# Second preparation of a chunked RWKV-7 layer with doubled buffers, group norm per tile, and another layout of pools and PSUM banks

## The chip, the cores and the metric

The kernel runs on one core of a Trainium2 chip. The metric is device time in microseconds (us), the median of several executions. Engines: PE multiplies matrices (PEld is its weight load), DVE is the vector engine, ACT the scalar engine, POOL is GpSimd, SP issues nearly all DMA transfers, in one queue.

## The reference, cut to what matters

The whole is one inference step of two layers: an RWKV-7 time mixing, a gated MLP, a windowed attention, a second gated MLP. Only the time mixing is touched, and the projection behind it:

```
r, k, v, decay, a, g = projections of the normed input        # g: gate, low rank, weights g1, g2
y, S_T = wkv7_scan(r, decay, k, v, -kk, kk * a, S0)           # 512 prompt tokens from S0 = 0,
                                                              # and 8 sample sequences of 4 tokens from given states
y = (y - mean) * rsqrt(var + eps)                             # group norm, per token and head of 64
y = y * ln_w + ln_b + sum(r * k * r_k) * v                    # the bonus
out = (y * g) @ w_o                                           # then x = x + out, and a norm
```

## The kernel before, in words

The 544 tokens (32 of the samples, 512 of the prompt) are two groups: group 0 has 288 columns (the first 256 prompt tokens and the samples), group 1 has 256. Function `rwkv` (L788) does the time mixing. Its first part makes r, k, v and the low-rank inputs by large matmuls. Then, per group g:

- `prep(g)` (L806) runs eight units, one for each pair of heads, by `unit_prep` (L397). The first half of a unit loads weights (l_raw) and r, k, v (`in0` to `in2`, from the spill), makes two tanh tiles `th0`, `th1` on ACT (L59 is the line of every operation that goes through the wrapper class `Lane`), a scan `cl` on DVE, its exponentials `dx` and `di`, `kk`, then the products `AR` (DVE), `BK` and `BE` (POOL). The second half makes the bonus from `pb` (a tile that shares the buffers of `cl`; matmul L485), transposes `BE` (L493), multiplies `AR` with `BK` (L498) and masks the result into `G` on DVE. The second half of unit m-1 stands in the program behind the first half of unit m.
- `inverses` (L505) inverts the triangular blocks of `G`: copies, a 32x32 transpose, sixty dependent DVE operations, transposes back, small matmuls.
- `scan(g)` calls `chain` (L561): four chunks of 64 tokens, one after the other through the state S. Per chunk: `own` (L570, matmuls L575, needed for the next chunk), the state's share (L598), `W` (L601, L602), matmuls L606, `UV` (L608, L609), the new state (L617, DVE L622 or L624), and `out` (L579, matmuls L583 and L587, ACT L589 into `yt`).
- `y_norm` (L715) is the group norm of the four `yt` tiles (and, for group 0, of two sample tiles `Ws`): sum and centring on DVE, squares on ACT, sum on DVE; then for all tiles together one scaling and one power -0.5 on POOL (tile `y_var`, 40 or 32 columns), then one POOL multiplication per tile.
- `outputs(g)` calls `y_out` (L740) for four pairs of heads: transposes of `yt` (L746), and for each of eight m the load of the bonus and of a gate weight (`lg_raw`, L759), its split into two parts (`lg_hi` on ACT, `lg_lo` on POOL), three matmuls (L98 to L100), two DVE operations, and a store to a spill in DRAM (`y_spill`, L773).

The order in `rwkv` (from L911 on): scan(0), prep(1) with `samples` (L630, the sample sequences, two halves) put in between, y_norm(0), inverses(1), scan(1), outputs(0), the final states, y_norm(1), outputs(1). Behind it, in `body` (L1527), `y_split` (L776) reads the spill back (`y_in`) and splits it into the operand tiles `y0` and `y1`, and a `Projection` (L945) multiplies by w_o: all eight blocks of group 0, a norm, all eight of group 1. Then the MLP.

The program is written in that order, but a scheduler with a timing model of its own fixes the order on each engine: what is ready may go ahead of earlier code. `Lane` (L51) bounds this: in each of four streams (even units, odd units, samples, y) an operation is placed only when the one 2 or 3 before it on its engine is done. Each engine and the SP queue then run in their fixed order. A tile name has a number of buffers (`bufs`); buffers of one name go round in the program's order, and a new use waits for the last reader of the old. Pools are stacks, from the left or the right end of SBUF: a pool opened after another was closed lies on its memory, and each of its tiles waits for the tiles that lay there.

Before the change `th0`, `th1`, `cl`, `di`, `kk` and `BK` have one buffer in prep(1); pool `us` (operands of the samples) lies on the left, `sp` (samples) and `yo` (y_norm and y_out) on the right, and behind them the next stage's weights `wp2` and `y0`, `y1`, `y_in` (pool `mp`) lie on the right too, from the same end. PSUM (8 banks): sm 1, cw 1, cp 3, pp 3; in the projection and the MLP pp 2, mm 6.

Of the kernel before, what the change touches and what calls it, by code (L numbers as in the profile page):

```python
# [9 lines left out]
F = mybir.dt.float32  # L10
FR = mybir.dt.float32r
AF = mybir.ActivationFunctionType
OP = mybir.AluOpType
# [54 lines left out]
def run(gen):  # L68
    for _ in gen:
        pass  # L70
# [558 lines left out]

def samples(c, hb, b, sp):  # L630

# [9 lines left out]
    for j in range(4):  # L641
        vk = sp.tile([128, 4, 128], F, name="st", bufs=2)
# [16 lines left out]
    nc.scalar.activation(V, rows(ps), AF.Copy)  # L659
    BE = sp.tile([128, 4, 128], F, name="st", bufs=2)  # L660
    for j in range(4):
# [6 lines left out]
    nc.scalar.activation(BT, rows(ps, 128), AF.Copy)  # L668
    W = sp.tile([128, 4, 64], F, name="Ws", bufs=2)
    ps = c.sm()  # L670
# [14 lines left out]
    WU = sp.tile([128, 4, 64], F, name="WUs", bufs=1)  # L685
    nc.vector.tensor_scalar(WU, W, c.parity[:, 2:3], None, op0=OP.mult)
    U = WU
# [27 lines left out]
def y_norm(c, yt, yo):  # L715

    nc = c.slow[3]
    var = c.small.tile([128, 40], F, name="y_var", bufs=1)
    parts = []
    for t in yt:  # L720
        k = t.shape[1] // 64
        at = parts[-1][2] if parts else 0
        parts.append((t.rearrange("p (x v) -> p x v", v=64), at, at + k))
    for t, lo, hi in parts:
        k = hi - lo
        s = c.small.tile([128, 8], F, name="y_sum", bufs=2)
        nc.vector.reduce_sum(s[:, :k], t, axis=AX.X)
        nc.vector.scalar_tensor_tensor(t, s[:, :k].unsqueeze(2).to_broadcast([128, k, 64]), -1.0 / 64, t,
                                       op0=OP.mult, op1=OP.add)
        sq = yo.tile([128, 8, 64], F, name="y_sq", bufs=1)  # L730
        nc.scalar.activation(sq[:, :k], t, AF.Square)
        nc.vector.reduce_sum(var[:, lo:hi], sq[:, :k], axis=AX.X)
    w = parts[-1][2]
    nc.vector.tensor_scalar(var[:, :w], var[:, :w], 1.0 / 64, 64e-5, op0=OP.mult, op1=OP.add)
    nc.gpsimd.tensor_tensor(var[:, :w], var[:, :w], c.mhalf[:, :w], OP.pow)
    for t, lo, hi in parts:
        nc.gpsimd.tensor_tensor(t, t, var[:, lo:hi].unsqueeze(2).to_broadcast([128, hi - lo, 64]), OP.mult)


def y_out(c, g, jj, yt, ys, yo):  # L740
# [13 lines left out]
    for par in range(2):  # L754
        m = 2 * jj + par
        bn = yo.tile([128, NA], F, name="bonus_in", bufs=2)
        nc.sync.dma_start(bn[:, :n], c.bd[:, m, g0:g0 + n])
        lg = yo.tile([128, 128], F, name="lg_raw", bufs=1)
        nc.sync.dma_start(lg, a["rwkv_g2"][0, :, m * 128:(m + 1) * 128])  # L759
        lhi = yo.tile([128, 128], FR, name="lg_hi", bufs=1)  # L760
        llo = yo.tile([128, 128], FR, name="lg_lo", bufs=1)
        split(c, lhi, llo, lg, nc.gpsimd, nc)
# [25 lines left out]
def rwkv(c):  # L788
    nc, tc, a = c.nc, c.tc, c.a
    with ExitStack() as rx:  # L790
# [51 lines left out]

        px, py, rp, rq, ra, rb = (ExitStack() for _ in range(6))
        pm = px.enter_context(c.pool("ps_mm", space=PSUM))
# [41 lines left out]
        px.close()  # L886
        us = rx.enter_context(c.pool("us"))
        u0 = rx.enter_context(c.pool("u0"))
# [30 lines left out]
        up = rx.enter_context(c.pool("up1"))  # L919
# [5 lines left out]
        sp = rx.enter_context(c.pool("sp", side="right"))  # L925
        yo = rx.enter_context(c.pool("yo", side="right"))
        scan(0)
        p1 = prep(1)
        next(p1)
        for hb in range(2):  # L930
            ysm.append(samples(c, hb, smp[hb], sp))
# [595 lines left out]
def body(tc, a, dbg=None, stop=None):  # L1527
# [7 lines left out]
    with ExitStack() as ctx:  # L1535
# [19 lines left out]
        def layers(layer, pr, rest, end, last=None):  # L1555
            with ExitStack() as px:
                psn = px.enter_context(c.pool("ps2", space=PSUM))
                c.pp = lambda: psn.tile([128, 512], F, name="pp", bufs=2)
                psp = px.enter_context(c.pool("ps3", space=PSUM))
                c.mm = lambda: psp.tile([128, 512], F, name="mm", bufs=6)  # L1560
                if last:
                    c.fin = px.enter_context(c.pool("fin"))
                rest()
                x = pr.x
                dump(c, ("x1", "x3")[layer], x)
                mx.close()
                ffn(c, layer, x, end, last)
                dump(c, ("x2", "x4")[layer], x)
# [101 lines left out]
```

## Time and profile before

| | |
|---|---|
| three runs | 2258.44, 2258.45, 2260.52 us (median 2258.45) |
| the profiled execution, own time | 2257.57 us |
| its span, first to last instruction | 2255.5 us |
| granted TensorE clock, mean | 0.942 of full speed |
| busy over the span | PE 91%, PEld 85%, DVE 52%, ACT 40%, POOL 27% |

The span is cut into stretches in the rows below. A busy share over the whole says little here, since PE is full for most of the time and half idle between about 270 and 593 us, where the time mixing's chains run. A wait is read as: which engine stood idle before an instruction, and what released it.

### The profile page before, as it was taken

The numbers are of one execution on the slowest core, as the hardware profiler recorded it, in microseconds if no ns is written. First come the engines' busy times: TensorE is split into PE (matmuls) and PEld (weight loads), VectorE is DVE, ScalarE is ACT, GpSimd is POOL, SyncE is SP. The second block draws the span as 40 slices with busy tenths as digits, with TensorE's granted clock in tenths as the row PEclk, the third lists the DMA queues.
The fourth block names the chain that finished last, engine by engine and source line by source line (L and its number), as shares of the span: only waits on it lengthen the run. The fifth ranks groups of instructions, "written<-read, shape, count | busy, mean of one in ns | idle before, by whom it ended". The sixth has DMA issues, their size and how long they took to land. (4 is left out here: it accounts for less than half of the span.)

```text
span 2255.5 us, 48553 instructions
## 1 busy us (share of the span) xinstructions
PE 2049.3 (91%) x19286; PEld 1926.7 (85%) x19286; DVE 1173.4 (52%) x2402; ACT 895.2 (40%) x1867; POOL 612.4 (27%) x786
## 2 busy tenths in 40 slices
PE   6889848746699999999899999999999999999998
PEld 5888746535699999999889888888888799999998
DVE  6776876665474443325445445454454664344323
ACT  6555523312354444324333333333333354444323
POOL 5874815523132222002111111111111132222101
PEclk9989968658699999999999999999999999999999
DMA  4236511214542332336444444354444443233233
GB/s 155 90 110 202 154 37 44 56 23 118 149 137 82 90 91 83 96 109 179 122 134 129 127 136 130 106 140 124 127 126 124 135 135 90 82 93 88 86 89 108
DMA packets 445053, 250.15 MB, mean 111 GB/s; under 512 B 43578, under 2 KB 436954, under 8 KB 444698
## 3 DMA queue, kind: packets, MB, share of 16 engines
q1 hardware_dynamic: 444826, 247.05, 38.6%
q8 instruction: 151, 2.47, 0.5%
q14 instruction: 76, 0.62, 0.1%
HBM read 202.74 MB, written 30.85 MB: 104 GB/s over the span
## 5 line engine op out<-in xcount | busy, mean ns | idle before, releaser
L99 PE MATMUL mm<-xn,w_hi 128*128 128x256 f32 (+1 forms) x2688 | 788.8, 294 | 2.0 <-DVE xn L1009 0.9
L98 PE MATMUL mm<-xn,w_hi 128*128 128x256 f32 (+1 forms) x2688 | 784.5, 293 | 3.7 <-ACT xn L1008 3.7
L100 PE MATMUL mm<-xn,w_lo 128*128 128x256 f32 (+1 forms) x2688 | 780.5, 291 | 0.0
L75 DVE TENSOR_TENSOR w_lo<-w_raw,w_hi 128x512 fp32r<-128x512 f32 (+1 forms) x575 | 434.7, 758 | 561.9 <-ACT w_hi L74 550.8
L74 ACT ACTIVATE w_hi<-w_raw 128x512 fp32r<-128x512 f32 (+1 forms) x575 | 355.8, 620 | 551.1 <-PE mm L99 488.7
L98 PEld LDWEIGHTS mm<-xn,w_hi 128*128 128x128 f32 x2688 | 509.4, 190 | 9.9 <-ACT xn L1008 4.3
L99 PEld LDWEIGHTS mm<-xn,w_hi 128*128 128x128 f32 x2688 | 510.0, 190 | 6.9 <-issue 2.8
L100 PEld LDWEIGHTS mm<-xn,w_lo 128*128 128x128 f32 x2688 | 509.0, 190 | 3.1 <-issue 3.0
L98 PE MATMUL mm<-act,w_hi 128*128 128x288 f32 (+1 forms) x704 | 200.6, 289 | 1.6 <-ACT y_out L1041 1.6
L1195 POOL TENSOR_TENSOR qk_raw<-qk_raw,rope 128x1088 f32<-128x1088 f32 x24 | 86.2, 3594 | 420.4 <-DMA qk_sw<-qk_raw 384.1
L99 PE MATMUL mm<-act,w_hi 128*128 128x288 f32 (+1 forms) x704 | 200.1, 288 | 0.0
L100 PE MATMUL mm<-act,w_lo 128*128 128x256 f32 (+1 forms) x704 | 198.9, 289 | 0.0
L98 PEld LDWEIGHTS mm<-act,w_hi 128*128 128x128 f32 x704 | 131.9, 189 | 1.7 <-ACT y_out L1041 1.7
L99 PEld LDWEIGHTS mm<-act,w_hi 128*128 128x128 f32 x704 | 131.6, 188 | 0.0
L147 POOL TENSOR_TENSOR acc<-acc,sq_t 128x288 f32<-128x288 f32 (+1 forms) x56 | 46.7, 834 | 310.8 <-ACT sq_t L146 310.7
L100 PEld LDWEIGHTS mm<-act,w_lo 128*128 128x128 f32 x704 | 130.8, 188 | 0.0
L100 PE MATMUL mm<-mx,w_lo 128*128 128x288 f32 (+1 forms) x384 | 114.3, 300 | 3.4 <-DVE w_lo L75 3.3
L98 PE MATMUL mm<-mx,w_hi 128*128 128x288 f32 (+1 forms) x384 | 114.1, 299 | 1.7 <-ACT w_hi L74 1.6
L99 PE MATMUL mm<-mx,w_hi 128*128 128x288 f32 (+1 forms) x384 | 113.5, 297 | 0.0
L100 PEld LDWEIGHTS mm<-mx,w_lo 128*128 128x128 f32 x384 | 74.6, 195 | 6.5 <-DVE w_lo L75 5.8
L1280 ACT ACTIVATE scores<-scores,sm_m 128x512 f32<-128x512 f32 (+3 forms) x80 | 50.4, 631 | 72.0 <-DVE sm_m L1279 69.9
L98 PEld LDWEIGHTS mm<-mx,w_hi 128*128 128x128 f32 x384 | 75.1, 196 | 2.8 <-ACT w_hi L74 2.3
(363 smaller groups left out, 3277.5 us busy)
## 6 DMA issues: line engine op xcount, KB each, us to landing
w_raw<-ffn_w_up SPq DMA_DIRECT2D x176, 256.0 KB
w_raw<-attn_w_in SPq DMA_DIRECT2D x144, 256.0 KB
w_raw<-ffn_w_down SPq DMA_DIRECT2D x90, 256.0 KB
w_raw<-rwkv_w_rkv SPq DMA_DIRECT2D x80, 256.0 KB
qk_sw<-qk_raw SPq DMA_DIRECT2D x96, 136.0 KB
cache_k<-cache_k_w SPq DMA_DIRECT2D x96, 128.0 KB
cache_v<-cache_v_w SPq DMA_DIRECT2D x96, 128.0 KB
w_raw<-rwkv_w_o SPq DMA_DIRECT2D x32, 256.0 KB
```

Source lines behind the costliest of these rows:

```text
L74: (nc or c.nc).scalar.activation(out_hi, src, AF.Copy)
L75: lo_engine.tensor_tensor(out_lo, src, out_hi.bitcast(F), OP.subtract)
L98: nc.tensor.matmul(ps, hi, xhi(i), start=first and i == 0, stop=False)
L99: nc.tensor.matmul(ps, hi, xlo(i), start=False, stop=False)
L100: nc.tensor.matmul(ps, lo, xhi(i), start=False, stop=last and i == len(w) - 1)
L147: nc.gpsimd.tensor_tensor(acc, acc, t[:, :n], OP.add)
L1195: nc.gpsimd.tensor_tensor(raw, raw, c.rope[:, 0:1].to_broadcast([128, 2, NT]), OP.mult)
L1280: nc.scalar.activation(s[:, :w], s[:, :w], AF.Exp, scale=0.125, bias=m[:, 1:2], accum_out=m[:, 2:3])
```

## The change

It does the following:

- prep(1) gets two buffers for `th0`, `th1`, `cl`, `di`, `kk` (c.ub) and for `BK` (c.ubk).
- In `samples`: `um` shares the buffers of `st`, which get three instead of two (before: `um` two of its own); `Ws` moves to the longer-lived pool `sa`; the masking `WUs` goes from DVE to ACT.
- `y_norm` does scaling, power and multiplication tile by tile; `var` is a small tile with two buffers.
- `y_out`: bonus_in 4 buffers instead of 2, lg_raw 3 instead of 1, lg_hi and lg_lo 2 instead of 1.
- PSUM in this part: sm 2, `cw` and `cp` together 3, pp 3. The projection gets its own banks in `layers` (mm 5, pp 3, closed before the MLP opens mm 6, pp 2).
- SBUF: `us` goes to the right end; `us`, `sp` and prep(1)'s pool `up1` are closed before y_norm(0), and `yo` is opened after that on the left, where `up1` was.

```diff
-    W = sp.tile([128, 4, 64], F, name="Ws", bufs=2)
+    W = keep.tile([128, 4, 64], F, name="Ws", bufs=2)
...
-    nc.vector.tensor_scalar(WU, W, c.parity[:, 2:3], None, op0=OP.mult)
+    nc.scalar.activation(WU, W, AF.Copy, scale=c.parity[:, 2:3])
...
-        um = sp.tile([128, 8, 64], F, name="um", bufs=2)
+        um = sp.tile([128, 8, 64], F, name="um", tag="st", bufs=3)
...
-        so = sp.tile([128, 4, 128], F, name="st", bufs=2)
+        so = sp.tile([128, 4, 128], F, name="st", bufs=3)
...
+        t = t.rearrange("p (x v) -> p x v", v=64)
+        var = c.small.tile([128, 8], F, name="y_var", bufs=2)[:, :k]
+        s = c.small.tile([128, 8], F, name="y_sum", bufs=2)[:, :k]
+        nc.vector.reduce_sum(s, t, axis=AX.X)
+        nc.vector.scalar_tensor_tensor(t, s.unsqueeze(2).to_broadcast([128, k, 64]), -1.0 / 64, t, op0=OP.mult, op1=OP.add)
         sq = yo.tile([128, 8, 64], F, name="y_sq", bufs=1)
         nc.scalar.activation(sq[:, :k], t, AF.Square)
...
+        nc.vector.reduce_sum(var, sq[:, :k], axis=AX.X)
+        nc.vector.tensor_scalar(var, var, 1.0 / 64, 64e-5, op0=OP.mult, op1=OP.add)
+        nc.gpsimd.tensor_tensor(var, var, c.mhalf[:, :k], OP.pow)
+        nc.gpsimd.tensor_tensor(t, t, var.unsqueeze(2).to_broadcast([128, k, 64]), OP.mult)
...
-        bn = yo.tile([128, NA], F, name="bonus_in", bufs=2)
+        bn = yo.tile([128, NA], F, name="bonus_in", bufs=4)
...
-        lg = yo.tile([128, 128], F, name="lg_raw", bufs=1)
+        lg = yo.tile([128, 128], F, name="lg_raw", bufs=3)
...
-            so = sp.tile([128, 4, 128], F, name="st", bufs=2)
+            so = yo.tile([128, 4, 128], F, name="p_st", bufs=1)
...
-        us = rx.enter_context(c.pool("us"))
+        us = ru.enter_context(c.pool("us", side="right"))
...
-        c.sm = lambda: pq.tile([128, 512], F, name="sm", bufs=1)
-        c.cw = lambda: pq.tile([128, 512], F, name="cw", bufs=1)
-        c.cp = lambda: pq.tile([128, 512], F, name="cp", bufs=3)
+        c.sm = lambda: pq.tile([128, 512], F, name="sm", bufs=2)
+        c.cw = c.cp = lambda: pq.tile([128, 512], F, name="cp", bufs=3)
...
-        c.ubk = 1
+        c.ub, c.ubk = 2, 2
...
         run(p1)
+        ux.close()
+        rs.close()
+        ru.close()
+        yo = rx.enter_context(c.pool("yo"))
         y_norm(c, st[0]["yt"] + ysm, yo)
...
+                with c.pool("ps2", space=PSUM) as psn:
+                    c.mm = lambda: psn.tile([128, 512], F, name="mm", bufs=5)
+                    c.pp = lambda: psn.tile([128, 512], F, name="pp", bufs=3)
+                    rest()
```

## Rows read from the trace of the kernel before

**Rows 1.** Busy us by stretch: PE, PEld, DVE, ACT, POOL; PEclk, DMA share, GB/s.
```profile
318.00:357.00 39.00, 35.14 (x717) 30.99 (x712) 22.94 (x36) 16.64 (x36) 17.73 (x25) 0.95 0.09 20
357.00:467.00 110.00, 83.69 (x431) 62.78 (x430) 63.59 (x103) 36.65 (x80) 66.36 (x89) 0.67 0.26 58
467.00:506.00 39.00, 12.95 (x281) 11.97 (x281) 31.46 (x76) 4.51 (x7) 1.01 (x3) 0.53 0.08 13
506.00:549.00 43.00, 37.18 (x700) 33.25 (x700) 24.93 (x49) 10.87 (x24) 10.02 (x13) 0.87 0.23 68
549.00:593.00 44.00, 13.76 (x46) 9.72 (x44) 12.40 (x24) 6.76 (x15) 13.51 (x13) 0.52 0.56 162
593.00:622.00 29.00, 28.79 (x195) 28.51 (x196) 20.40 (x38) 17.65 (x39) 5.64 (x6) 0.90 0.66 183
622.00:1005.00 383.00, 381.78 (x3041) 381.09 (x3040) 166.28 (x322) 158.25 (x281) 79.99 (x136) 1.00 0.34 98
```

**Rows 2.** Timeline, 547 to 594 us: start, duration, instruction, idle time before and its releaser.
```profile
547.02 1.41 DVE L624 TENSOR_TENSOR S<-cp,SD 64x512 f32<-64x512 f32 x2 [1.59 <-PE cp L617]
...
549.18 0.60 ACT L838 ACTIVATE st<-sm 128x512 f32<-128x512 f32 x1 [0.80 <-PE sm L836]
...
561.28 0.48 PE L746 MATMUL pp<-ca,yt 128*128 128x128 f32 x1 [0.52 <-POOL yt L59]
...
577.40 0.31 ACT L59 ACTIVATE lg_hi<-lg_raw 128x128 fp32r<-128x128 f32 x1 [2.56 <-DMA lg_raw<-rwkv_g]
...
580.23 0.31 ACT L59 ACTIVATE lg_hi<-lg_raw 128x128 fp32r<-128x128 f32 x1 [2.52 <-DMA lg_raw<-rwkv_g]
...
589.53 0.32 SPq L773 DMA_DIRECT2D y_spill<-bonus_in  x1
589.90 0.43 SPq L783 DMA_DIRECT2D y_in<-y_spill  x1
...
593.16 0.85 PE L98 MATMUL mm<-y,w_hi 128*128 128x288 f32 x2 [4.21 <-ACT y L74]
```

**Rows 3.** Groups by line, 549 to 593 us: busy us, mean ns, idle before, releaser.
```profile
L98 PE MATMUL pp<-hg,lg_hi 128*128 128x256 f32 x8 | 4.6, 579 | 16.2 <-ACT lg_hi L59 16.2
...
L59 ACT ACTIVATE lg_hi<-lg_raw 128x128 fp32r<-128x128 f32 x7 | 2.2, 309 | 22.5 <-DMA lg_raw<-rwkv_g 22.5
...
L59 DVE TENSOR_REDUCE y_var<-y_sq 128x8 f32<-128x512 f32 x1 | 0.7, 685 | 0.8 <-ACT y_sq L59 0.8
```

**Rows 4.** Groups by line on POOL, 357 to 467 us (columns as in rows 3).
```profile
L59 POOL TENSOR_TENSOR y_var<-y_var,mhalf 128x40 f32<-128x40 f32 x1 | 6.8, 6772 | 0.0
...
L59 POOL TENSOR_TENSOR BK<-th,di 128x256 f32<-128x256 f32 x7 | 5.1, 732 | 34.6 <-PE pp L498 21.4 <-PE pp L416 13.2
...
L59 POOL TENSOR_TENSOR yt<-yt,y_var 128x512 f32<-128x512 f32 x4 | 4.0, 1032 | 0.0
```

**Rows 5.** Timeline of single instructions in the second preparation (columns as in rows 2).
```profile
370.30 0.47 ACT L59 ACTIVATE th<-pp,hpar 128x256 f32<-128x256 f32 x1 [5.44 <-PE pp L498]
...
428.46 4.04 POOL L59 TENSOR_TENSOR Ss<-Ss,s_dend 128x512 f32<-128x512 f32 x4
...
429.20 4.81 DVE L59 TENSOR_SCALAR WUs<-Ws,cb 128x256 f32<-128x256 f32 x1
...
430.54 0.47 ACT L59 ACTIVATE th<-pp,hpar 128x256 f32<-128x256 f32 x1 [1.15 <-POOL Ss L59]
```

**Rows 6.** Timeline of the first and second scan (columns as in rows 2).
```profile
329.08 1.14 DVE L59 SCALAR_TENSOR_TENSOR yt<-y_sum,yt 128x512 f32<-128x512 f32 x1
...
333.77 1.15 PE L575 MATMUL cw<-UV,G 128*64 128x64 f32 x32
...
337.07 1.39 DVE L624 TENSOR_TENSOR S<-cp,SD 64x512 f32<-64x512 f32 x2 [2.51 <-PE cp L617]
...
337.73 1.10 PE L587 MATMUL cp<-UV,G 128*64 128x64 f32 x32
...
524.98 1.97 PE L575 MATMUL cw<-UV,G 128*64 128x64 f32 x32
```

More of the change, by code (lines that the diff above doesn't have):

```diff
@@ L627, in chain, with samples @@
         out(ch, S)
-def samples(c, hb, b, sp):
+def samples(c, hb, b, sp, keep):
     nc, a = c.slow[2], c.a
@@ L641, in samples @@
     for j in range(4):
-        vk = sp.tile([128, 4, 128], F, name="st", bufs=2)
+        vk = sp.tile([128, 4, 128], F, name="st", bufs=3)
         for x in range(2):
@@ L659, in samples @@
     nc.scalar.activation(V, rows(ps), AF.Copy)
-    BE = sp.tile([128, 4, 128], F, name="st", bufs=2)
+    BE = sp.tile([128, 4, 128], F, name="st", bufs=3)
     for j in range(4):
@@ L717, in y_norm @@
     nc = c.slow[3]
-    var = c.small.tile([128, 40], F, name="y_var", bufs=1)
-    parts = []
     for t in yt:
         k = t.shape[1] // 64
[L722 to L729, printed above, removed]
+        t = t.rearrange("p (x v) -> p x v", v=64)
[3 more added lines that the diff above has]
+        nc.vector.scalar_tensor_tensor(t, s.unsqueeze(2).to_broadcast([128, k, 64]), -1.0 / 64, t, op0=OP.mult, op1=OP.add)
         sq = yo.tile([128, 8, 64], F, name="y_sq", bufs=1)
         nc.scalar.activation(sq[:, :k], t, AF.Square)
[L732 to L737, printed above, removed]
+        nc.vector.reduce_sum(var, sq[:, :k], axis=AX.X)
+        nc.vector.tensor_scalar(var, var, 1.0 / 64, 64e-5, op0=OP.mult, op1=OP.add)
+        nc.gpsimd.tensor_tensor(var, var, c.mhalf[:, :k], OP.pow)
+        nc.gpsimd.tensor_tensor(t, t, var.unsqueeze(2).to_broadcast([128, k, 64]), OP.mult)
 def y_out(c, g, jj, yt, ys, yo):
@@ L755, in y_out @@
         m = 2 * jj + par
-        bn = yo.tile([128, NA], F, name="bonus_in", bufs=2)
+        bn = yo.tile([128, NA], F, name="bonus_in", bufs=4)
         nc.sync.dma_start(bn[:, :n], c.bd[:, m, g0:g0 + n])
-        lg = yo.tile([128, 128], F, name="lg_raw", bufs=1)
+        lg = yo.tile([128, 128], F, name="lg_raw", bufs=3)
         nc.sync.dma_start(lg, a["rwkv_g2"][0, :, m * 128:(m + 1) * 128])
-        lhi = yo.tile([128, 128], FR, name="lg_hi", bufs=1)
-        llo = yo.tile([128, 128], FR, name="lg_lo", bufs=1)
+        lhi = yo.tile([128, 128], FR, name="lg_hi", bufs=2)
+        llo = yo.tile([128, 128], FR, name="lg_lo", bufs=2)
         split(c, lhi, llo, lg, nc.gpsimd, nc)
@@ L841, in states @@
                 nc.sync.dma_start(a["o_p_wkv"][0, 0, 8 * hb + h:8 * hb + 8:2].rearrange("j v k -> v j k"), so[q, :, q])
-        px, py, rp, rq, ra, rb = (ExitStack() for _ in range(6))
+        px, py, rp, rq, ra, rb, ru, rs = (ExitStack() for _ in range(8))
+        us = ru.enter_context(c.pool("us", side="right"))
         pm = px.enter_context(c.pool("ps_mm", space=PSUM))
@@ L913, in rwkv @@
         pq = rx.enter_context(c.pool("ps_pp", space=PSUM))
-        c.sm = lambda: pq.tile([128, 512], F, name="sm", bufs=1)
-        c.cw = lambda: pq.tile([128, 512], F, name="cw", bufs=1)
-        c.cp = lambda: pq.tile([128, 512], F, name="cp", bufs=3)
+        c.sm = lambda: pq.tile([128, 512], F, name="sm", bufs=2)
+        c.cw = c.cp = lambda: pq.tile([128, 512], F, name="cp", bufs=3)
         c.pp = c.iv = lambda: pq.tile([128, 512], F, name="pp", bufs=3)
         sa = rx.enter_context(c.pool("sa"))
-        up = rx.enter_context(c.pool("up1"))
-        c.ubk = 1
+        ux = ExitStack()
+        up = ux.enter_context(c.pool("up1"))
+        c.ub, c.ubk = 2, 2
         c.W = sa.tile([128, 512], F, name="W")
@@ L924, in rwkv @@
             nc.gpsimd.memset(t, 0.0)
-        sp = rx.enter_context(c.pool("sp", side="right"))
-        yo = rx.enter_context(c.pool("yo", side="right"))
+        sp = rs.enter_context(c.pool("sp", side="right"))
         scan(0)
@@ L930, in rwkv @@
         for hb in range(2):
-            ysm.append(samples(c, hb, smp[hb], sp))
+            ysm.append(samples(c, hb, smp[hb], sp, sa))
             for _ in range(4):
@@ L1556, in layers @@
             with ExitStack() as px:
[L1557 to L1560, printed above, removed]
                 if last:
                     c.fin = px.enter_context(c.pool("fin"))
-                rest()
+                with c.pool("ps2", space=PSUM) as psn:
+                    c.mm = lambda: psn.tile([128, 512], F, name="mm", bufs=5)
+                    c.pp = lambda: psn.tile([128, 512], F, name="pp", bufs=3)
+                    rest()
                 x = pr.x
@@ L1566, in layers @@
                 mx.close()
+                psp = px.enter_context(c.pool("ps3", space=PSUM))
+                c.mm = lambda: psp.tile([128, 512], F, name="mm", bufs=6)
+                c.pp = lambda: psp.tile([128, 512], F, name="pp", bufs=2)
                 ffn(c, layer, x, end, last)
```

## The prediction

> **What bounds the kernel now.** I read the stretches first, to see where the matrix engine waits [rows 1]. From 622 to 1005 us PE is busy 381.78 of 383 us at the full clock (2.4 GHz); the stretch is matmul work, and nothing short of fewer matmuls shortens it. Ahead of it the time mixing's chains stand in a row: the first scan (318 to 357), the second preparation with the samples (357 to 467, 110 us, where no engine is full and PE is granted 0.67), the second inverse (467 to 506, DVE busy 31.46 of 39), the second scan (506 to 549), and a tail (549 to 593, PE busy 13.76 of 44 us at 0.52, near its lower level of 1.2 GHz). What these stretches give up moves all that follows to the left by as much.
>
> In the tail's timeline [rows 2] the last state update ends at 547.02 + 1.41 = 548.4 us, and the first matmul of the projection starts at 593.16: 44.7 us. Its operand is read back from 589.90 on, directly behind the last store of the output stage at 589.53, for group 0 too, whose rows were finished in the second scan: `y_in` and `y0` lie on the memory of `yo` and wait for its last tile. The output stage takes one step per 2.83 us (577.40 to 580.23), since `lg_raw` has one buffer: ACT stands idle 22.5 us over seven steps for that load, and PE 16.2 us for ACT behind it [rows 3]. It starts late as well, at 561.28 [rows 2], behind the whole group norm.
>
> In the second preparation the waits on POOL show a loop: POOL stands idle 34.6 us ahead of `BK` for matmuls, 21.4 of them for L498 of the unit before, the last reader of the only `BK` buffer [rows 4]. From unit 2's first tanh at 370.30 to unit 7's at 430.54 are 60.2 us, 12 us per unit [rows 5].
>
> **The change part by part.** The sum is made against the profiled execution, 2257.57 us, of which the span is 2255.5; the median of the runs shown is 2258.45, 0.9 above it.
>
> *Tail.* Now `y0` and `y_in` lie on `us`, `sp` and `up1`, dead since the end of prep(1), and the projection's five banks on `sm` and `cp`. So the read-back and split of group 0 can go into the second scan, behind outputs(0): eight steps at 2.83 are 23 us of its 43. First matmul: once the banks are free, that is when ACT has copied the first states at 549.18 [rows 2] for 0.6 us, so about 550 instead of 593.2, 43 us earlier. The output stage's PE work is then no longer in a gap but on the path: 13.76 us at a granted 0.52 are 7.2 at full clock [rows 1], leaving 36. DVE has 12.40 + 20.40 = 33 us of work for what is then a stretch of some 36 us [rows 1], so it will be late for PE at times; I take 4 us for that: **-32**. The deeper `lg` and bonus buffers and the norm per tile then lie beside the projection, and count only if it doesn't start early: the step falls from 2.83 to perhaps 1.5 us (ACT, POOL and PE work overlapped) for 11 us, and the norm behind the last chunk is one tile's power, 6772 ns / 40 columns x 8 = 1.4 us [rows 4], and one multiplication of 1.0, instead of everything up to 561.28: 6 us. So the tail lies between -17 and -38. The last copy of the states has one buffer for two and holds a bank for a DMA longer; the projection's second tile needs that bank only one block later: nothing. The weights' loads leave the place at 554 us where they stand among the output's loads; nothing counted.
>
> *Second preparation.* With two buffers the loop falls apart: unit m+1 may run up to `BK` while L498 of unit m is outstanding. What holds it next is an engine. POOL has 66.36 us, less 12 of group norm (6.8 + 4.0 and 1.2 for the small tiles) is 54; DVE 63.59, less 4 that `WUs` loses in its wait is 59; PE has 83.69 at the granted 0.67 and would have 56 at full clock [rows 1, 4]. The bounds are 0 (another wait takes over: `dx` and `BE` keep one buffer, SP's queue is in order with 32 sample transfers per half) and -47 (63 us). I take 86 us, near PE's busy time at the clock that the row shows, the highest of the three: **-24**.
>
> *Group norm of group 0.* Its DVE passes ran as early as 329.08, during the first scan [rows 6]. Now `y_sq` lies on `th0` of prep(1), so it can start only when unit 7 has used its `th0`, and it lands at the end of the preparation, ahead of the inverse in the program. Four tiles with three passes of 0.69 and one of 0.18, and two half as large, are 9.0 + 2.8 = 12 us of DVE [rows 3]. In its favour, the power no longer stands on POOL as one block of 6.8 us ahead of the last unit's `BE`. Bounds 0 (DVE is idle 46 of 110 us there) and +14 with the handovers; I take +4, and +2 for DVE operations of the samples' second half that now fall into the inverse's chain: **+6**. `um` in the buffers of `st` makes those samples slower, since it now waits for a store; the inverse's 39 us, with ACT and POOL all but idle [rows 1], hide it. `Ws` in another pool, and `WUs` on ACT: nothing on the path.
>
> *Scans.* `cw` had a bank of its own, so `own` of the next chunk (L575 at 333.77, 1.15 us) ran while `UV` was copied. From three shared banks it gets the one of a `pu` only after that copy, and then stands with L617 and `out` on PE under the state update of 1.39 us, which `out` already fills (L587 ends at 338.83, the update at 338.46) [rows 6]. Three per scan, six in all, at 1.15 (full clock) to 1.97 us (lower level, 524.98): 0 (placed behind the next chunk's first matmuls) to +12; I take **+6**.
>
> *Later banks* (mm 5 in the projection, a new pool in the MLP): PE is full in those stretches with three to five tiles in work; nothing, ±1. The first part's pools move by the size of `us`; ±3.
>
> Sum: 2257.57 - 32 - 24 + 6 + 6 = 2213.6, plus 0.9: **2214 us**.
>
> **A rule that speaks against it.** `WUs`, half as many elements as a DVE pass of 0.69 us [rows 3], took 4.81 us from 429.20, while POOL ran four multiplications for 4.04 us from 428.46 [rows 5]. The Trainium skill, page "SBUF — State Buffer", section "Who interferes with whom", says that a DVE operation with two SBUF inputs, or a copy-like one in its fast mode, and a GpSimd operation that reads SBUF exclude each other, the later one being blocked in full. By that rule, with this trace agreeing in one row, an overlapped preparation is worth less; that is the last rival below.
>
> **The rivals.**
> 1. *The preparation reaches its engines.* Two units in flight bring PE to the full clock, and 70 us are left of 110: -40, norm and scans +3 each, tail -36. 2257.57 - 66 + 0.9 = 2192. For it: the 34.6 us at `BK`. Against: the clock of 0.67.
> 2. *A wait takes the loop's place.* In-order SP loads, `dx`, `BE`: preparation 0. 2257.57 - 32 + 12 + 0.9 = 2238. For it: one shortage of buffers often hides the next; against: no other group shows 34.6 us.
> 3. *The projection doesn't start early*, so the change doesn't do what it says: a placement still ties `y0` or a bank to the output stage. Tail -17: 2257.57 - 17 - 24 + 12 + 0.9 = 2229.
> 4. *Slower: DVE and POOL block each other.* One loss like that of `WUs`, at least 4.1 us, on each of the two engines for each of seven units is 57 us, and the preparation gets longer, not shorter: 2257.57 + 57 + 12 - 32 + 0.9 = 2295. It decides from five such blocks on (20 us, the tail's 32 less 12). Against: POOL's operations now mostly take 0.7 to 1.0 us, so a block costs that much, and matmuls' results come from PSUM.
>
> **How the numbers follow.** Forecast 0.47, rival 1 0.20, rival 2 0.17, rival 3 0.08, rival 4 0.05, and 0.03 that gains and losses cancel. The forecast's own terms, each at its bounds but not all at once, give 2195 to 2232. The range takes in rivals 1 to 3 with some ±3 of the first part: 2187 to 2241, about 0.85. A measurement of this kernel tells about 0.2% (4.5 us) from no change. Faster by more: the forecast and rivals 1 to 3, 0.92; within: 0.03; slower: 0.05.
>
> **What would show it.** Right, step by step: the first matmul on `y` within a few us of the last state update, L746 of group 1 among projection matmuls, `y_in` of group 0 loaded inside the second scan; POOL's idle time ahead of `BK` well below 34.6 us and 8 to 9 us per unit; group norm on DVE at the end of the preparation; L575 behind the `UV` copies and some us more per scan; PE full from 550 us less the preparation's gain. Wrong: `y_in` behind the last output store again, a gap of PE ahead of the projection, the preparation still near 110 us, or DVE operations of several us beside POOL's.

## The result, and the profile after

The changed kernel takes 2229.47 us (median of 4 runs, 2227.63 to 2232.56), the kernel before 2258.44 beside it (4 runs): a ratio of 0.9872, 95% interval 0.9855 to 0.9889. The forecast was 2214, its range 2187 to 2241: the time lies inside, 15 us above the forecast, and on the 2229 us of rival 3. The profiled execution took 2228.93 us, its span is 2227.1 (before 2255.5).

I cut both traces at the same instructions, each mark one row of the timeline: the first 32x32 transposition (L523) of each inverse and the end of its last one (L535), the first `own` matmul (L575) of the second scan, the end of its last state update (L624), the first and last projection matmul on `y`, the first MLP matmul on `xn`. In us, for all kernels of this study (the names are explained below):

| kernel | preparation (inverse 0 to inverse 1) | inverse 1 | scan 1 | tail | projection | to the MLP |
|---|---|---|---|---|---|---|
| before | 185.35 | 27.70 | 42.60 | 44.73 | 52.88 | -1.50 |
| changed | 151.88 | 40.65 | 42.24 | 25.65 | 52.93 | 6.55 |
| changed, again (e11) | 154.04 | 40.70 | 45.55 | 23.76 | 53.46 | 6.47 |
| e1 old MLP banks | 155.96 | 40.73 | 41.93 | 24.08 | 53.36 | -1.50 |
| e2 y0 off yo | 152.44 | 34.03 | 56.42 | 21.38 | 50.65 | 7.08 |
| e3 y0 and banks | 151.82 | 33.87 | 57.04 | 3.51 | 62.96 | 12.30 |
| e4 banks only | 152.20 | 40.65 | 44.87 | 23.97 | 55.34 | 12.26 |
| e5 single buffers | 168.80 | 38.80 | 43.88 | 24.47 | 52.92 | 8.56 |
| e6 single output buffers | 156.19 | 40.41 | 47.36 | 37.31 | 52.77 | 7.69 |
| e7 norm in preparation | 163.94 | 34.31 | 44.61 | 23.74 | 52.54 | 7.56 |
| e8 e7 with old MLP banks | 165.84 | 34.46 | 45.21 | 23.41 | 53.04 | -1.51 |
| e9 own bank | 151.28 | 41.65 | 41.95 | 22.49 | 53.10 | 6.80 |
| e10 early projection | 153.01 | 40.74 | 49.36 | 1.42 | 59.94 | -1.61 |
| e12 single buffers, norm | 171.80 | 32.62 | 41.68 | 23.79 | 54.03 | 7.69 |

From the first two lines: -33.5 in the preparation, +13.0 in the inverse, -0.4 in the scan, -19.1 in the tail, 0 in the projection, +8.05 ahead of the MLP; with +2.2 before inverse 0 and +1.3 behind the first MLP matmul that is -28.4 us, the difference of the spans. The +1.3 is itself a sum: 12.2 us more ahead of the second MLP, 7.1 less inside the two MLPs and 3.9 less in the attention. The stretches in windows, of the changed kernel (columns as in [rows 1]): preparation without the first scan, inverse, second scan, tail, and the end of the projection.

```profile
358.92:438.10 79.18, 59.64 (x399) 45.18 (x397) 55.40 (x89) 35.05 (x78) 53.22 (x79) 0.84 0.33 77
438.10:478.75 40.65, 10.37 (x108) 6.14 (x109) 38.78 (x93) 6.51 (x13) 16.64 (x15) 0.50 0.36 87
487.52:529.76 42.24, 35.23 (x685) 32.13 (x685) 25.68 (x49) 10.19 (x23) 17.15 (x18) 0.87 0.22 66
529.76:555.41 25.65, 9.92 (x52) 8.06 (x48) 9.52 (x21) 4.53 (x11) 6.57 (x11) 0.62 0.62 184
...
610.00:620.00 10.00, 6.79 (x33) 6.20 (x33) 6.47 (x19) 3.98 (x10) 4.67 (x9) 0.66 0.36 105
```

The kernel before in windows at the same marks, preparation and inverse:

```profile
358.06:469.36 111.30, 83.09 (x424) 62.15 (x424) 64.84 (x105) 35.65 (x78) 66.42 (x88) 0.68 0.26 58
469.36:497.06 27.70, 4.13 (x85) 3.52 (x86) 25.70 (x67) 0.60 (x1) 0.00 (x0) 0.50 0.07 11
```

The preparation shrinks from 111.3 to 79.2 us, and PE is granted 0.84 instead of 0.68 there; the inverse holds 13.1 us more of DVE, all of its 13 us. The tail is to be read beside [rows 2]. The timeline of the changed kernel:

```profile
528.35 1.41 DVE L624 TENSOR_TENSOR S<-cp,SD 64x512 f32<-64x512 f32 x2 [1.12 <-PE cp L617]
...
536.68 0.48 PE L739 MATMUL pp<-ca,yt 128*128 128x128 f32 x1 [5.39 <-POOL yt L59]
...
548.02 0.41 PE L100 MATMUL pp<-hg,lg_lo 128*128 128x256 f32 x1
555.41 0.85 PE L98 MATMUL mm<-y,w_hi 128*128 128x288 f32 x2 [6.98 <-ACT y L74]
...
547.27 4.65 SPq L766 DMA_DIRECT2D y_spill<-bonus_in  x3
551.97 0.43 SPq L776 DMA_DIRECT2D y_in<-y_spill  x1
```

The output stage's last transposition of its first four comes 536.68 - 529.76 = 7 us behind the scan (13 before, [rows 2]), its steps are shorter, but `y_in` of group 0 is again loaded directly behind the last store. The projection does not overlap with anything. And it loses time at its other end, in the changed kernel's PE timeline:

```profile
608.17 0.28 PE L100 MATMUL mm<-y,w_lo 128*128 128x256 f32 x1
611.89 1.01 PE L114 MATMUL pp<-ones,acc 128*128 128x1 f32 x4 [3.44 <-POOL acc L147]
613.93 0.69 PE L122 MATMUL pp<-ca,rs_b 128*128 128x128 f32 x2 [1.03 <-POOL rs_b L119]
...
614.89 0.61 PE L98 MATMUL mm<-xn,w_hi 128*128 128x288 f32 x1
```

Before, the first MLP matmul stood 1.5 us ahead of the last of the projection, and MLP work filled the norm of group 1. Now the MLP's pool `ps3` opens only when `ps2` is closed behind that norm: in these 6.55 us PE runs nothing but a few small matmuls, and the matmuls that follow run at the lower level of 1.2 GHz at first (granted 0.50 from 614.89 to 617.9, 0.44 us for 288 columns at 615.3; granted 1.00 and 0.30 us from there on).

### The profile page after: what moved, and what is told of

It is laid out like the page before. It is cut to its first block, busy times and chain, and to the rows that moved or that the text cites. A ratio compares the mean times of both kernels' runs of the same rounds, so it can differ in the third digit from the quotient of the medians.

```text
span 2227.1 us, 48630 instructions
## 1 busy us (share of the span) xinstructions
PE 2025.3 (91%) x19286; PEld 1907.8 (86%) x19286; DVE 1173.6 (53%) x2408; ACT 895.1 (40%) x1869; POOL 610.5 (27%) x794
## 5 line engine op out<-in xcount | busy, mean ns | idle before, releaser
L1092 POOL TENSOR_SCALAR cvo<-gate 128x2 f32<-128x2 f32 x44 | 19.7, 448 | 214.6 <-ACT gate L1083 214.6
```

What stands on the lines that cost most here:

```text
L1092: nc.gpsimd.tensor_scalar(cvo[:, 0:2], ge[:, 560:562], 1.0, None, op0=OP.mult)
```

## The experiments

Each was timed beside the kernel before on the same chip, and the median of that kernel was 2262 to 2267 us; so ratios are compared, or kernels timed side by side. e11 is the changed kernel once more: 0.9869 (0.9843 to 0.9894), and its stages lie within 3.4 us of the first trace.

> The changed kernel once more, beside the two others. If the stages repeat, each of those read above (preparation 151.9, inverse 40.65, second scan 42.2, tail 25.65, projection 52.9, gap ahead of the MLP 6.6 us) comes out within 2 us, and what differs lies in the attention, whose stretch was between 747.7 and 762.3 us in kernels in which no line of it was changed; if it doesn't, differences of that size between single profiles say nothing.

Four of its six stages repeat within 2 us, the preparation within 2.2, scan 1 only within 3.3. The attention (from the first copy of its q, k, v out of PSUM to its last output transposition) took 749.4 us in the first trace and 756.2 in this one, and 747.7 to 762.3 over all kernels, none of which changes it: a total from one trace is good to some 10 us only, and the stages are what is read.

**The MLP's banks (e1).** In `layers`:

```
-                with c.pool("ps2", space=PSUM) as psn:
-                    c.mm = lambda: psn.tile([128, 512], F, name="mm", bufs=5)
-                    c.pp = lambda: psn.tile([128, 512], F, name="pp", bufs=3)
-                    rest()
+                psn = px.enter_context(c.pool("ps2", space=PSUM))
+                c.pp = lambda: psn.tile([128, 512], F, name="pp", bufs=2)
+                psp = px.enter_context(c.pool("ps3", space=PSUM))
+                c.mm = lambda: psp.tile([128, 512], F, name="mm", bufs=6)
+                rest()
```

> The changed kernel with the MLP's banks as they were (two for pp and six for mm, opened together before the projection). Theory A: of the 37.75 us by which the first projection matmul came earlier, 9.3 us were given back between 600 and 640 us because the MLP's pool opens only when the projection's is closed: TensorE stands idle from 608.2 to 614.4 but for two short groups, and then runs at half clock to 618. With the old pools the MLP's first matmuls fill the norm of group 1 again: 2229.5 - 9 = 2220 us (2218 to 2223). Theory B: the gap comes from weights and norm operations that are simply late for a projection that starts 37 us earlier; then the old pools change nothing: 2228 to 2231 us, and the gap stays near 6 us.

2222.71 us, ratio 0.9813 (0.9780 to 0.9846), about 0.6% below the changed kernel's. The gap is gone (-1.50 us), in a window of e1:

```profile
610.00:620.00 10.00, 8.87 (x68) 8.41 (x68) 5.80 (x18) 3.81 (x10) 4.24 (x6) 1.00 0.36 102
```

PE is busy 8.87 of 10 us at full clock where it was 6.79 at 0.66. Theory A holds. The same code runs ahead of the second MLP: from the attention's last output transposition to the second MLP's first gate copy the changed kernel takes 39.7 us, e1 27.9, before 27.5. The new banks give back some of it inside the MLPs (first one 413.4 us against 415.4, the rest of the second one 405.4 against 406.5), so they cost 8.05 + 11.8 - 3.1 = 16.8 us by these stages, and some 13 by the ratios (0.6% of 2229).

**Why the projection starts late (e2, e3, e4).** e2 closes the inverse's pool ahead of `yo`, so that `yo` moves down and `y0` lies on none of it:

```
-        si = rx.enter_context(c.pool("si"))
+        si = ux.enter_context(c.pool("si"))
...
-        y_norm(c, st[0]["yt"] + ysm, yo)
-        inverses(c, st[1]["G"], si)
+        with c.pool("si1") as si:
+            inverses(c, st[1]["G"], si)
+        yo = rx.enter_context(c.pool("yo"))
+        y_norm(c, st[0]["yt"] + ysm, yo)
```

> The changed kernel with the inverses' tiles in a pool of their own behind the second preparation, closed before yo is opened; yo moves down by 13 KB and y0 no longer lies on it. The group norm of group 0 then stands behind the second inverse. Theory A (two ties: y0 lies on yo, and the projection's banks belong to a pool that the output stage still uses): the read-back and split of group 0 move into the second scan, but the projection's first matmul stays behind the last output matmul and is only some 4 us earlier (555.4 becomes 551); the second inverse gets up to 13 us shorter and the scan takes the norm's 12 us of DVE, so 2229.5 - 4 - (0 to 13): 2212 to 2226 us. Theory B (y0 on yo was the only tie): the projection starts near 531 beside the output stage, another 13 to 17 us: 2197 to 2212 us.

0.9875 (0.9835 to 0.9916), no better than the changed kernel, and above both ranges. One row on the tile `y_in`, and two of PE's timeline, of e2:

```profile
L776 SPq DMA_DIRECT2D y_in<-y_spill x8: 319/430/437, 505.4 to 528.3; - x8
```

```profile
558.41 0.41 PE L100 MATMUL pp<-hg,lg_lo 128*128 128x256 f32 x1
558.62 0.44 PE L98 MATMUL mm<-y,w_hi 128*128 128x288 f32 x1
```

Group 0 is read back inside the scan (480.82 to 537.24), and the first projection matmul still follows the last output matmul: the tail is 4.3 us shorter, as theory A said, and there is a second tie. The norm now lies in the scan, which gets 14.2 us longer, while the inverse gets 6.6 shorter. e3 adds a pool of its own for the `cp` banks, closed ahead of y_norm(1), with the projection's `mm` on it; e4 does that alone:

```
-        c.cw = c.cp = lambda: pq.tile([128, 512], F, name="cp", bufs=3)
+        rc = ExitStack()
+        pc = rc.enter_context(c.pool("ps_cp", space=PSUM, side="right"))
+        c.cw = c.cp = lambda: pc.tile([128, 512], F, name="cp", bufs=3)
...
+        rc.close()
         y_norm(c, st[1]["yt"], yo)
...
-                with c.pool("ps2", space=PSUM) as psn:
-                    c.mm = lambda: psn.tile([128, 512], F, name="mm", bufs=5)
+                with c.pool("ps2", space=PSUM) as psn, c.pool("ps4", space=PSUM, side="right") as psm:
+                    c.mm = lambda: psm.tile([128, 512], F, name="mm", bufs=3)
```

> As the run before, and the scan's three cp banks in a pool of their own, closed behind the second scan, on which the projection's mm tiles lie (three instead of five). Theory A (two ties): only now does the projection run beside the output stage: first projection matmul within 3 us of the last state update, and against the run before 10 to 17 us less (24.4 us between the last state update and the first projection matmul, less 7 us of output matmuls at full clock, less some 4 us in which DVE is late). Theory B (y0 alone was the tie): the same time as the run before within 3 us. A third possibility: the output stage's steps get slower behind the projection's matmuls on TensorE, group 1 is late for the projection, and the gain falls to 0 to 5 us.

> The changed kernel with the cp banks in a pool of their own and the projection's mm tiles on them, y0 still on yo. Theory A (both ties have to go): the read-back of group 0 stays behind the last output step, and the time stays at 2229.5 +- 3 us. Theory B (the banks were the only tie): 12 to 17 us less, 2212 to 2218 us.

The starts are as theory A has them: 3.51 us behind the last update in e3, 23.97 in e4. The times are not: 0.9882 (0.9848 to 0.9917) and 0.9917 (0.9885 to 0.9950), e3 as e2 (the size of the third possibility) and e4 slower. Three banks instead of five cost by themselves: in e4 the projection takes 55.34 instead of 52.93 us, and 12.26 instead of 6.55 us are lost ahead of the MLP. That eats what e3's early start brings (72.0 us from the last update to the last projection matmul in e2, 66.5 in e3).

**Both ties without the costs (e10).** As e3, but with the norm ahead of the inverse, its squares on the inverse's tile `XT`, three banks for the first eight `mm` of the first projection only, then three more, and the MLP's banks ready before:

```
+        with c.pool("si1") as si:
+            y_norm(c, st[0]["yt"] + ysm, lambda: si.tile([128, 32, 32], F, name="XT", bufs=1).rearrange("p n t -> p (n t)")[:, :512].rearrange("p (x v) -> p x v", v=64))
+            inverses(c, st[1]["G"], si)
...
+                psm = px.enter_context(c.pool("ps4", space=PSUM, side="right"))
+                psp = px.enter_context(c.pool("ps3", space=PSUM))
+                turn = [8 * layer]
+                def mm():
+                    turn[0] += 1
+                    return (psm if turn[0] <= 8 or turn[0] % 2 else psp).tile([128, 512], F, name="mm", bufs=3)
```

> What the runs so far point to, together: inverse tiles in a pool of their own below yo, so that y0 lies on nothing of the output stage; the group norm of group 0 ahead of the second inverse as in the changed kernel, with its squares on the inverse's tile XT; the cp banks in a pool of their own on which the first eight mm tiles of the first projection lie; the MLP's banks as they were. Theory A (the ties of y0 and of the banks were two, and with both gone the projection fills the output stage's idle TensorE time): inverse 38 to 42 us, second scan 43 to 47 (it takes the read-back's split), first projection matmul within 5 us of the last state update, last one 64 to 68 us after that update (78.6 in the changed kernel, 77.4 with the old MLP banks alone), MLP without a gap: 2208 to 2216 us. Theory B (TensorE's time beside the output stage is worth nothing, because group 1 is late by as much): the last projection matmul 74 to 79 us after the last update, 2217 to 2224 us, as with the old MLP banks alone.

2204.15 us, ratio 0.9730 (0.9704 to 0.9756) beside 0.9869 of the changed kernel on the same chip: it beats both. Its windows, second scan and from the last update to the last projection matmul:

```profile
486.49:535.85 49.36, 38.48 (x700) 34.92 (x700) 29.81 (x61) 13.93 (x33) 19.28 (x21) 0.83 0.30 83
535.85:597.21 61.36, 57.18 (x450) 55.14 (x447) 45.19 (x86) 32.26 (x72) 21.31 (x27) 1.00 0.73 210
```

```profile
536.11 1.09 PE L829 MATMUL sm<-ca,S 128*128 128x128 f32 x8
...
537.27 0.29 PE L98 MATMUL mm<-y,w_hi 128*128 128x288 f32 x1
```

Those 61.36 us were 77.2 in the changed kernel beside it (23.76 + 53.46): 15.9 less, and the scan pays 3.8 (7.1 against the first trace) for the read-back's split. PE is busy 57.18 of the 61.36 us at the full clock, DVE 45. Theory A holds; the scan is 2.4 us above what it said and the projection's end 2.6 us earlier. The time is 4 us below its range, and why is open: ahead of the second MLP 28.5 us are left of 41.3, but e1, whose time that range builds on, had 27.9 there already; the attention took 750.5 us in this trace and 757.5 in e1's, a difference of that size.

**The preparation (e5, e7, e12).** e5 sets `c.ub, c.ubk = 1, 1` in prep(1); e7 puts the norm's squares on the inverse's dead tile `X`, so that the norm of group 0 can run inside the preparation; e12 does both; e8 is e7 with e1's banks:

```
-        c.ub, c.ubk = 2, 2
+        c.ub, c.ubk = 1, 1
...
-        sq = yo.tile([128, 8, 64], F, name="y_sq", bufs=1)
+        sq = yo.tile([128, 32, 32], F, name="X", bufs=1).rearrange("p n t -> p (n t)")[:, :512].rearrange("p (x v) -> p x v", v=64)
...
-        y_norm(c, st[0]["yt"] + ysm, yo)
+        y_norm(c, st[0]["yt"] + ysm, si)
```

> The changed kernel with one buffer each in the second preparation (the tiles th, cl, di, kk and BK). Theory A (the doubled buffers own the preparation's gain): from the first DVE transposition of inverse 0 to that of inverse 1 were 185.35 us before and 151.88 in the changed kernel; this run is back at 182 to 188, and the time is 2229.5 + 33 = 2262 us (2256 to 2266). Theory B (a part of the gain is the group norm of group 0, 7 us of power on POOL and 12 us of DVE, that has left the preparation, and the samples' third buffer): the stretch comes back to 165 to 178 us and the time to 2243 to 2255 us.

> The changed kernel with the squares of the group norm (y_sq) on the inverse's tile X, which is dead between the two inverses, instead of in yo, which lies on the preparation's tiles: the norm of group 0 may run inside the second preparation again. Theory A (the norm's passes inside the second inverse are why that got 13 us longer, 27.7 to 40.65 us from its first transposition to its last): the inverse is back at 28 to 30 us, the preparation hides most of the norm, and the time is 2216 to 2222 us. Theory B (the norm costs the preparation what it costs the inverse, since DVE and POOL hinder each other there): the inverse gets shorter, the preparation longer by as much, and the time stays at 2227 to 2232 us.

> The changed kernel with both undone in the second preparation: single buffers, and the norm's squares on the inverse's tile X, so that the norm of group 0 runs in there. From inverse 0 to inverse 1 were 151.9 and 154.0 us in two profiles of the changed kernel, 168.8 with single buffers, 163.9 with the norm, 185.35 before. Theory A (buffers 17 us, norm 12 us, each by itself, and some 4 us for the samples): 179 to 183 us, inverse 34 us. Theory B (both wait for the same engines, so together they cost little more than the larger): 168 to 174 us, and the rest to 185 is the samples' third buffer and the order of the norm's blocks. Theory C (they sharpen each other): 185 us or more. Time 12 us more than with single buffers, less 6 in the inverse, by theory A.

e5: 0.9956 (0.9941 to 0.9970), the preparation 168.8 us. With its code unchanged (changed, e11, e1, e4, e6) the preparation took 151.9 to 156.2 us, so the buffers are worth 13 to 17 of the 33.5 us: theory B. The gain lies among the units: from the first `BK` to the end of the last are 97.5 to 102.0 us with two buffers and 118.6 in e5, and some 4 us of it are lost again between there and the inverse. The loop at `BK` is back, in the waits of POOL from 358 to 467 us in e5:

```profile
POOL BK L59 <- PE pp L498: 20.1, 4, 7.5
POOL BK L59 <- PE pp L416: 6.2, 2, 4.3
```

The same view of the changed kernel has no wait of `BK`; its longest are

```profile
POOL y_var L59 <- DVE y_var L59: 12.5, 4, 9.0
POOL BE L59 <- PE pp L493: 7.2, 1, 7.2
```

e7: 0.9916 (0.9899 to 0.9932), some 10 us slower than the changed kernel by the ratios and outside both ranges. By the stages the norm costs the preparation 8 to 12 us with two buffers and spares the inverse 6: theory B, with a loss of 2 to 6. The rest of the 10 us is in none of these two stages, and e8 below doesn't repeat it. e12: 0.9941 (0.9918 to 0.9964), preparation 171.8 us, theory B: with single buffers the norm finds room and costs 3 us, no more than traces differ. So 13.5 us of the 185.35 are neither. Most of them lie behind the last `BK`. POOL's timeline of the kernel before

```profile
452.98 0.73 POOL L59 TENSOR_TENSOR BK<-tk,di 128x256 f32<-128x256 f32 x1
453.67 6.77 POOL L59 TENSOR_TENSOR y_var<-y_var,mhalf 128x40 f32<-128x40 f32 x1
460.42 1.03 POOL L59 TENSOR_TENSOR BE<-BK,dc 128x512 f32<-128x512 f32 x1
```

of e12, which has the single buffers too and the norm tile by tile

```profile
447.69 0.75 POOL L59 TENSOR_TENSOR BK<-tk,di 128x256 f32<-128x256 f32 x1
448.52 1.04 POOL L59 TENSOR_TENSOR BE<-BK,dc 128x512 f32<-128x512 f32 x1
```

and of the changed kernel:

```profile
424.73 0.91 POOL L59 TENSOR_TENSOR BK<-tk,di 128x256 f32<-128x256 f32 x1
425.71 1.37 POOL L59 TENSOR_TENSOR BE<-BK,dc 128x512 f32<-128x512 f32 x1
```

The power of all tiles stood in one block of 6.77 us between the last unit's `BK` and `BE`, for which transposition, `G` and the inverse wait. Tile by tile there is no such block. From the end of the last `BK` to the inverse are 15.65 us before and 6.54 in e12: 9.1 of the 13.5 us, 6.6 of them the wait of `BE`. The units ahead of it are 5.0 us shorter (128.4 and 123.4 us from the first `BK` to the end of the last); the samples' buffers and `WUs` on ACT are what is left of the change there, were not tried by themselves, and stay open. In the changed kernel the block is gone as well, but only 3.2 us of it show (12.46 us from the last `BK` to the inverse): the transposition starts 4.7 us behind `BE` there, 1.9 before.

> Both edits together: the norm's squares on the inverse's tile X, and the MLP's banks as they were. If the two gains are of different stretches they add up: 9 us from the MLP's banks and what the norm alone gives in this call, 2207 to 2213 us by theory A of both. If the projection's stretch gives back what it gets earlier, the sum stays 3 us or more behind that.

e8: 2217.4 us, 0.9803 (0.9788 to 0.9818), 25 us below e7 beside it and within the interval of e1. It has e1's gap (-1.51) and e7's preparation and inverse, so the stages add: against e7 9.1 us less ahead of the first MLP and 14.8 less ahead of the second. The time stays above the 2207 to 2213 us, since the norm alone gained nothing; but here it cost nothing either (e1 0.9813, e8 0.9803). That the norm is no better off in the preparation is shown; how much worse, in the time, is not.

**The output stage's buffers (e6).** bonus_in 4 to 2, lg_raw 3 to 1, lg_hi and lg_lo 2 to 1.

> The changed kernel with the output stage's buffers as they were (bonus_in 2, lg_raw 1, lg_hi and lg_lo 1), the norm tile by tile kept. The tail from the last state update's end to the first projection matmul was 44.7 us before and 25.65 in the changed kernel. Theory A (the step of the output stage was bound by lg_raw's one buffer, eight steps of 2.83 us against 1.5): the tail is 36 to 39 us, the time 2240 to 2244 us. Theory B (the norm tile by tile carries the tail, the buffers hardly): tail 25 to 30 us, 2229 to 2234 us.

0.9980 (0.9963 to 0.9996), 24 us slower than the changed kernel by the ratios, where theory A said 10 to 15. The tail is 37.31 us, as theory A said. In the waits between last update and projection, e6

```profile
ACT lg_hi L59 <- DMA lg_raw<-rwkv_g: 23.0, 7, 5.9
```

and the changed kernel:

```profile
ACT lg_hi L59 <- DMA lg_raw<-rwkv_g: 7.7, 2, 4.6
```

The buffers are worth 37.31 - 25.65 = 11.7 us there, the other 44.73 - 37.31 = 7.4 I put down to the norm tile by tile, which no run takes back by itself (the output stage's fourth transposition comes 10.5 us behind the last update in e6, 12.9 before and 6.9 in the changed kernel); scan 1, in which outputs(0) runs, is 1.8 to 5.1 us longer without them. Some 5 us of the 24 are in none of these stages; the attention of this trace, 762.3 us, is the longest of all, and whether the edit has a part in that stays open.

**The scan's banks (e9).** sm 1, cw 1 of its own.

> The changed kernel with the scan's PSUM banks as they were (sm 1, cw 1 of its own, cp 3). The second scan, from its first own matmul to the end of its last state update, took 42.60 us before, 42.24 in the changed kernel, and 47.36 with the output stage's single buffers. Theory A (the shared bank costs the scans nothing, since own is placed in time in any case): second scan 41 to 43.5 us, time within 3 us of the changed kernel in this call. Theory B (the shared bank costs each scan some 3 to 5 us, which the deeper output buffers hide in the second one): second scan 37 to 40 us, and 3 to 8 us less in all. Theory C (samples or outputs need the second sm bank): scan or preparation get longer, 2 to 6 us more.

0.9869 (0.9847 to 0.9891), the same as the changed kernel beside it; scan 1 41.95 us. From the inverse's end, which is 11.7 us ahead of the scan here and 8.8 in the other kernels, to the last update are 53.7 us, against 51.0 and 54.3 in the two traces of the changed kernel. Theory A: the shared bank costs nothing that can be measured.

## Why the prediction was right, and where it was wrong

The time lay in the range, but the forecast's main term did not happen; the sum came close because the errors have both signs, and that is luck. So is the match with rival 3's 2229 to the microsecond: of its terms only the tail came out (-17, measured -19.1); its -24 and +12 were -33.5, +13.0 and nothing, and it had no term for the MLPs.

- **Tail, -32.** Wrong in its step "now `y0` and `y_in` lie on `us`, `sp` and `up1`, dead since the end of prep(1), and the projection's five banks on `sm` and `cp`". `y0` reached down over `yo` (e2), and the banks belonged to a pool that the output stage still used (e3, e4). Both ties had to go: each edit alone leaves the start at 21 or 24 us behind the last update, both together bring it to 3.5 and 1.4. What the step is worth by e10 is 15.9 us less 3.8. Against the kernel before, the stretch from the last update to the last projection matmul falls from 97.6 to 61.4 us in e10, and its scan is 6.8 us longer: -29.5 together. So the price of -32 was good for a placement that holds; that the read-back and split of group 0 cost the scan nothing was wrong. The fall-back in the same paragraph was right in both parts: 11 us for the step and 6 for the norm, against 11.7 (e6) and the 7.4 that remain. That is rival 3, tail -17, and it had 0.08; the chance was too small for a placement that I had not added up.
- **Second preparation, -24.** Right in mechanism (the wait at `BK` is gone, the clock went from 0.68 to 0.84), mis-sized: -33.5, of which the buffers, the cause that the forecast named, are 13 to 17 (e5). The power block of [rows 4] was named, under the norm, and not priced: some 6.6 us on the path with single buffers, by e12's trace, and 3.2 at most in the changed kernel.
- **Group norm of group 0, +6.** The step that failed is "it lands at the end of the preparation, ahead of the inverse": of its 24 DVE operations three ran in the first scan and three at the end of the preparation (from 434.75 us on); 18 ran inside the inverse, until 455.7 us, and that got 13.0 us longer, not 6. The groups of DVE inside the inverse, before

```profile
L531 DVE TENSOR_TENSOR XL<-XL,xt 128x30 f32<-128x30 f32 (+14 forms) x30 | 9.9, 332 | 1.0
L528 DVE TENSOR_TENSOR xt<-XL 128x30 f32<-128x30 f32 (+14 forms) x30 | 9.9, 331 | 1.0
```

and in the changed kernel:

```profile
L528 DVE TENSOR_TENSOR xt<-XL 128x30 f32<-128x30 f32 (+14 forms) x30 | 11.7, 389 | 0.7
L531 DVE TENSOR_TENSOR XL<-XL,xt 128x30 f32<-128x30 f32 (+14 forms) x30 | 10.9, 364 | 0.6
L59 DVE TENSOR_REDUCE y_var<-y_sq 128x8 f32<-128x512 f32 (+1 forms) x5 | 2.9, 573 | 0.0
L75 DVE TENSOR_TENSOR w_lo<-w_raw,w_hi 128x512 fp32r<-128x512 f32 x4 | 2.8, 689 | 0.5 <-ACT w_hi L74 0.5
L59 DVE TENSOR_SCALAR y_var<-y_var 128x8 f32<-128x8 f32 (+1 forms) x5 | 2.1, 415 | 0.0
```

  The norm's groups in there sum to 9.3 us (with sums, centring and `Ws`), `w_lo` of the next weights to 2.8, and the chain's own sixty operations got 22.6 - 19.8 = 2.8 longer (neighbours overlap a little, so the parts are more than the whole). Without the norm, in e7, 6.3 of the 13 us go, so the norm itself was worth about the 6 forecast; the other 6.7 are `w_lo`, more of the samples and the output stage, and waits, where the forecast had 2. The chain leaves DVE almost no gap (25.70 of 27.70 us), so what is put on DVE there counts almost in full; my +4 allowed for work that runs beside it. Yet by e7 it is no worse a place than the preparation, where the same norm cost 8 us or more.
- **Scans, +6.** Right in the order, wrong in the price: nothing that e9 can measure, the lower of the two bounds. In the second scan of the changed kernel `own` does stand behind L617 and under the state update:

```profile
509.62 1.10 PE L575 MATMUL cp<-UV,G 128*64 128x64 f32 x32
510.04 1.40 DVE L624 TENSOR_TENSOR S<-cp,SD 64x512 f32<-64x512 f32 x2
```

  It ends at 510.7, ahead of the update (511.4); `out` behind it ends later by as much, and the next chunk's L598 starts 0.9 us behind the update. Over the three steps of this scan that wait is 2.0 us, before 1.0: about 1 us where the forecast had 3 per scan.
- **Later banks, 0 ± 1.** Wrong: "PE is full in those stretches with three to five tiles in work" looked at the tiles and not at the moment at which the second pool opens. 8.05 us at the first MLP, and 11.8 at the second, against 3.1 gained inside the MLPs.
- **First part ± 3:** +2.2 us, no more than traces of kernels with the same first part differ (283.2 to 288.8 us up to inverse 0).
- **The other rivals.** Rival 1 (its terms add up to -70 and 2188 us, not -66 and 2192): the clock rose and the preparation gained more than forecast, but no engine is full (PE 59.64 of 79.18, DVE 55.40, POOL 53.22). Rival 2: no wait took the whole place of the loop. Rival 4, DVE and POOL blocking each other: seen, and worth about 4 us, not 57. In the inverse, DVE and POOL of the changed kernel:

```profile
444.12 1.01 DVE L59 TENSOR_SCALAR y_var<-y_var 128x8 f32<-128x8 f32 x1
445.65 1.08 DVE L528 TENSOR_TENSOR xt<-XL 128x84 f32<-128x84 f32 x1
446.65 0.41 DVE L59 TENSOR_REDUCE y_sum<-Ws 128x4 f32<-128x256 f32 x1
446.98 0.23 DVE L531 TENSOR_TENSOR XL<-XL,xt 128x84 f32<-128x84 f32 x1
```

```profile
444.04 1.06 POOL L59 TENSOR_TENSOR um<-Vs,cb 128x512 f32<-128x512 f32 x1
445.07 1.56 POOL L59 TENSOR_TENSOR yt<-yt,y_var 128x512 f32<-128x512 f32 x1
446.59 1.64 POOL L59 TENSOR_TENSOR y_var<-y_var,mhalf 128x8 f32<-128x8 f32 x1
```

  An `xt` that starts at 445.65 ends at 446.73, when POOL's multiplication ends (446.63); its partner `XL` of the same size takes 0.23. The Trainium skill, page "SBUF — State Buffer", section "Who interferes with whom", has this as an exclusive lock; the trace agrees for POOL's multiplications of 512 columns. Four such operations of 1.0 to 1.1 us stand in the inverse up to 453 us. The 2.8 us by which the chain's sixty operations got longer are all in six that ran beside POOL's multiplications or its `lg_lo`, and two scalings of `y_var` lost 1.3 us more; with that the estimate for the inverse is 4 us. The 4.1 us of [rows 5] took more than the four multiplications named there: two `BK` products followed on POOL without a gap, until 433.86, and `WUs` ended at 434.01.

## What to carry to other kernels

A stage that is to start early on "dead" memory needs every tie cut, SBUF and PSUM, and a new pool of banks should lie wholly on a pool that was closed before; add up the tile sizes to the last kilobyte, and look in the trace for the first load of the new stage. A pool that is opened only when the one before is closed is a barrier, also for work that had filled a gap there. What is moved into a chain that already fills its engine counts almost in full, and a long block on a slow engine (here the power) is cheap or dear by what stands behind it.

## What was not expected of the hardware

POOL's power of 128x8 does not hold up DVE: while it ran from 446.59 to 448.23, the `XL` product above took 0.23 us, though both read two SBUF operands, so the lock named above does not show here; beside POOL's multiplications such products took 1.0 us and more. And one program repeats less well than its median suggests: the ten runs of e5 span 2245.9 to 2259.6 us, those of e6 2250.9 to 2265.3, and two traces of the changed kernel differ by 6.8 us in the attention alone.
